# Column sums of head and layer norms in float32r from split sources, the split a stage ahead

## The chip, the cores and the metric

The kernel runs on one core of a Trainium2 chip. The metric is the device time of one execution in microseconds. Five engines work beside each other, each through its own instructions in a fixed order: TensorE (PE, matrix products), VectorE (DVE), ScalarE (ACT), GpSimd (POOL) and SyncE (SP, which issues transfers). Semaphores join them.

## The reference, cut to what matters

One step of a decoder layer, for 512 prompt tokens and 8 samples (520 columns), in float32. The norms that the change touches are these:

```
qa = rms_norm(qa.reshape(bsz, t, A_HEADS, 2, A_HD), lw['a_qnorm_g'])      # 4 heads x 2 x 64
ka = rms_norm(ka.reshape(bsz, t, A_HEADS, 2, A_HD), lw['a_knorm_g'])
o = diff_attention(...)                                                   # 4 heads, values of 128
o = rms_norm(o, lw['a_subln_g']) * (1.0 - lam_init)
yc = silu(layer_norm(conv_c, lw['c_ln_g'], lw['c_ln_b'])) @ lw['w_c_out'] # 256 channels
dvn = layer_norm(dv, lw['d_ln_g'], lw['d_ln_b'])                          # 256 channels
q = rms_norm((h2 @ lw['w_xq'])..., lw['x_qnorm_g'])                       # cross attention, 4 heads of 128
mk = rms_norm((mem_n @ w_xk)..., x_knorm_g)                               # 4 heads, 256 memory rows
```

Around them stand the products with w_in, w_o, w_up and w_down, the attention over the prompt, a paged attention of the samples over 2048 past tokens, two convolutions and a gated branch.

## The kernel before

Channels lie on the 128 partitions and tokens along the free axis, so a norm sums over partitions. That is a product on TensorE: `colsum` multiplies a matrix of ones (`ones`, or `blk` with two blocks of 64) in float32 with the squares, for two halves of 260 columns, and every partition gets the sum. `rsqrt` (L249 to L255) makes the reciprocal deviation of it with four ACT and two DVE instructions.

The large products are float32r in three passes: each weight tile is split in a high part (`wh`, a cast on ACT, L179) and a low part (`wl`, a subtraction on DVE, L180), each activation likewise by `hilo` (L143 and L144). A tile of 128 output channels is 48 products of 260 columns (L219, into one of only two PSUM tiles `g`). The weights' tiles come as one stream, and the work on the results is written as generators: each `yield` ends a stage, and `advance` moves all that are under way by one stage behind every tile of the stream. So the order on each engine is set when the program is made: a tile's 48 products, then the small products of the stages that are due, then the next tile.

For a head norm, stage one empties the `g` tile with a multiplication (L433, `zmul`) and squares on ACT (L438, `square`), and stage two sums (L242), makes `rsqrt`, scales (L444) and splits q or k for the attention. `values` (L646 to L656) does the same for the attention's output with 256 columns (sum at L653), `post_mk` for the memory's keys (sum at L1081). `branch_c` and `branch_d` are layer norms: `center` (L785, L787) subtracts the mean from two tiles and squares, a yield, then the variance. `decode` mixes in the paged products: at L500 four products of 32 columns of weights each for one page, one for each head, and L549 for the values. L702 writes a head's queries for it (`qz`). L1196 does the same for the samples in cross attention, from `xz`.

Of the kernel before, what the change touches and what calls it, by code (L numbers as in the profile page):

```python
# [17 lines left out]
P = 128  # L18
D = 1024
NT = 520          # tokens: 512 of the prompt, then 8 samples  # L20
NP = 512
NS = 8
H2 = 260          # half of the tokens, one PSUM bank each
# [14 lines left out]
TB = 10  # L38
SLOPES = [2.0 ** (-2.0 * (i + 1)) for i in range(4)]

# order of the column tiles of w_in in the stream (tile = 128 columns)
ZQ, ZK, ZV, ZBX, ZBB, ZBC, ZCA, ZCG, ZDU, ZDV, ZG = 0, 4, 8, 12, 14, 16, 18, 20, 22, 24, 26

# columns of the packed per-partition vectors
# [10 lines left out]
# columns of the packed constants  # L55
# [40 lines left out]
def layer(ctx: ExitStack, tc: tile.TileContext, I: dict, O: dict):  # L96
# [12 lines left out]
    # ---------------------------------------------------------------- helpers  # L109
# [31 lines left out]
    def hilo(src, hi, lo):  # L141
        """hi + lo = src exactly; hi is rounded to what one pass of the tensor engine carries."""
        S.copy(hi, src)  # L143
        V.tensor_tensor(out=lo, in0=src, in1=f(hi), op=ALU.subtract)  # L144
# [20 lines left out]
    def weights(name, i):  # L165
        """the split column tile i of a matrix; the next one of the stream is begun first."""
        while len(ahead) < LA and order:
            ahead.append((order[-1], split_weights(*order.pop())))
        (n, j), w = ahead.pop(0)
        assert (n, j) == (name, i), (n, j, name, i)  # L170
        return w
# [11 lines left out]
    def first_weights():  # L183
        """the first tile of the stream, in parts that come between those of x"""
        j = order.pop()
        src = I[j[0]][j[1]].rearrange("p (k c) -> p k c", k=KT)
        w = wp.tile([P, KT, P], F32, tag="w", name="w", bufs=WB[0])
        wh = wp.tile([P, KT, P], F32R, tag="wh", name="wh", bufs=WB[1])
        wl = wp.tile([P, KT, P], F32R, tag="wl", name="wl", bufs=WB[2])
        ahead.append((j, (wh, wl)))  # L190
        n = KT // PARTS
        parts = [slice(i * n, i * n + n) for i in range(PARTS)]
        for sl in parts:
            SP.dma_start(out=w[:, sl], in_=src[:, sl])
            yield
        for sl in parts:
            tc.keep_in_program_order(S.copy(wh[:, sl], w[:, sl]))
            free.add(V.tensor_tensor(out=wl[:, sl], in0=w[:, sl], in1=f(wh)[:, sl], op=ALU.subtract).ins.name)
            yield
# [3 lines left out]
    def pin():  # L203
        """what VectorE has been given since the last sums were taken up stays behind that."""
        traced = nc.cur_bb.bb.instructions
        if evac[0] is not None:
            for i in traced[evac[1]:]:
                if i.engine == evac[0].engine and i.name not in free and i is not evac[0]:
                    tc.add_manual_dep(i, evac[0].name, mybir.DependencyInfo(
                        mybir.DependencyClass.NoSync, mybir.DependencyReason.DATA), reason="pin")  # L210
        evac[1] = len(traced)
# [3 lines left out]
    def mm3(outs, wh, wl, xh, xl, first, last):  # L215
        """outs: [(psum region, moving slice)], adds w^T x in three passes."""
        for n, (w, x) in enumerate(((wh, xh), (wh, xl), (wl, xh))):
            for o, sl in outs:
                m = PE.matmul(o, lhsT=w, rhs=x[sl], start=first and n == 0, stop=last and n == 2)  # L219
        return m  # L220
# [7 lines left out]
    def gemm(ps, W, xs, first=True, last=True, k0=0, apart=False):  # L228
        """both halves of the tokens; apart: one after the other"""
# [6 lines left out]
    def colsum(mat, srcs):  # L236
        """mat^T (sum of srcs over partitions) in float32: two halves with their columns."""
        out = []
        for sl in (slice(0, H2), slice(H2, NT)):
            ps = mtile()  # L240
            for i, s in enumerate(srcs):
                PE.matmul(ps[:, 0:H2], lhsT=mat, rhs=s[:, sl], start=i == 0, stop=i == len(srcs) - 1)  # L242
            out.append((ps[:, 0:H2], sl))
        return out

    def rsqrt(src, n, v, y, a):
        """v = (src / n + EPS) ** -0.5, with one Newton step: v (3 - x v^2) / 2."""
# [19 lines left out]
    def rstd(mat, srcs, n, y, v=None):  # L267
        """the reciprocal deviations from column sums; y is scratch."""
        v, a = v if v is not None else T(), T()
        rsqrt(colsum(mat, srcs), n, v, y, a[:, 0:NT])  # L270
        return v

    # ---------------------------------------------------------------- constants
# [15 lines left out]
    ident, ones, blk = cv("ident"), cv("ones"), cv("blk")  # L289

    # ---------------------------------------------------------------- x: split, norm
# [5 lines left out]
    for i in range(WARM):          # the array's clock rises while the first loads come in  # L297
# [45 lines left out]
    def parameters():  # L343
        """the little columns made from the parameters"""
# [20 lines left out]
    # ---------------------------------------------------------------- the stream of products  # L365
    pending, flows, fresh = [], [], [False]

    def behind():
        """keeps a product that waits for others out of the way of the column tiles before it."""
        return tc.issue_after(PE_last[0].ins)  # L370

    def onward(ps):
        """a stage of each, behind the newest column tile; returns those that go on"""
# [3 lines left out]
    def advance():  # L377
        """the newest sums are taken up, then what is left of the older ones goes a stage on."""
# [10 lines left out]
    def go():  # L389
        """a stage of everything"""  # L390
# [6 lines left out]
    def flush():  # L397
        """everything that is left"""
# [3 lines left out]
    def take(post):  # L402
        """what follows on a tile's sums is begun behind the next tile."""
# [5 lines left out]
    def run(name, i, src, post, steps=0, k0=0, W=None, apart=False):  # L409
        """one column tile"""  # L410
# [7 lines left out]
    def pair(names, src, posts):  # L418
        """the first two column tiles, together while the rows of src come in"""
# [16 lines left out]
    def square(z):  # L436
        sq = T()
        S.activation(sq, z, AF.Square)  # L438
        return sq

    def headnorm(z, sq, mat, n, g):
        """z * g * rsqrt(mean over the rows of mat's blocks)"""
        y = rstd(mat, [sq], n, sq)
# [15 lines left out]
    # ---------------------------------------------------------------- paged decode attention  # L459
    last = []  # L460

    def fetch(dst, src, i):
        """dst = the page that entry i of the page table names."""
# [9 lines left out]
    def decode():  # L473
# [33 lines left out]
        # the new token's own score  # L507
# [76 lines left out]
    # ---------------------------------------------------------------- attention over the prompt  # L584
    def scores(h, qts):
        """the scores of 128 queries each; the two halves of a head in banks of their own"""
# [14 lines left out]
    def difference(h, qt, ps):  # L601
        """of the two softmaxes"""
# [20 lines left out]
    def turned(h, qt, d):  # L623
        """the keys of one tile of queries on the partitions"""
# [13 lines left out]
    def values(h, pr, dh, dl):  # L638
        """times v, and the norm of the head"""
# [10 lines left out]
        S.activation(sq[:, 0:256], ps[:, 0:256], AF.Square)  # L650
        yield
        ps = mtile()
        PE.matmul(ps[:, 0:256], lhsT=ones, rhs=sq[:, 0:256], start=True, stop=True)  # L653
# [9 lines left out]
    def attention():  # L663
        """a stage a tile: the scores of some queries, the turning of those before, their values, their norm"""
# [18 lines left out]
    def post_q(h):  # L683
        def post(ps):
# [9 lines left out]
            qn = headnorm(z, sq, blk, 64, sc[:, 0:1])  # L694
# [10 lines left out]
    def post_k(h):  # L705
        def post(ps):
# [3 lines left out]
            kn = headnorm(z, sq, blk, 64, col("gk"))  # L710
# [25 lines left out]
    # ---------------------------------------------------------------- branch B  # L736
# [43 lines left out]
    def center(ys, ps):  # L780
        """subtracts the mean over the 256 channels of two tiles; returns the squares."""
# [7 lines left out]
        return sq  # L789

    # ---------------------------------------------------------------- branch C
# [51 lines left out]
    # ---------------------------------------------------------------- branch D  # L843
    def sigmoid(y, x, scale=1.0):
        """between exponentials, whose table is called back"""
# [22 lines left out]
    def branch_d():  # L868
        sq = center(dv, colsum(ones, dv))
        yield  # L870
        r = rstd(ones, sq, 256, sq[0])
# [65 lines left out]
    def branch_c():  # L937
        convstep(31)
        lnexp()
        sq = center(yc, colsum(ones, yc))  # L940
        yield
        r = rstd(ones, sq, 256, sq[0])
# [13 lines left out]
    # ---------------------------------------------------------------- gates and merge  # L956
# [85 lines left out]
    # ---------------------------------------------------------------- memory K/V of the prompt  # L1042
# [31 lines left out]
    def post_mk(h):  # L1074
        def post(ps):
            t, sq = T(), T()
            V.tensor_tensor(out=t[:, 0:256], in0=ps[:, 0, 0:256], in1=Rm, op=ALU.mult)
            S.activation(sq[:, 0:256], t[:, 0:256], AF.Square)
            yield
            ps = mtile()  # L1080
            PE.matmul(ps[:, 0:256], lhsT=ones, rhs=sq[:, 0:256], start=True, stop=True)  # L1081
# [21 lines left out]
    def memvalues(q):  # L1103
        """a quarter of the products for the values of all heads, the tokens on the partitions"""
# [25 lines left out]
    # ---------------------------------------------------------------- w_o, first residual  # L1130
    def residual(c, ps, base, acc, g):
        """x = base + ps; its split times the gain g; its squares into acc."""
# [30 lines left out]
    # ---------------------------------------------------------------- cross attention  # L1163
# [6 lines left out]
    def post_xq(h):  # L1170
        def post(ps):
# [14 lines left out]
            qn = headnorm(z, sq, ones, 128, sc[:, 2:3])  # L1186
# [24 lines left out]
    def samples():  # L1211
        """the samples against their memories"""
# [36 lines left out]
    def cross(h):  # L1249
        """the prompt against its memory"""  # L1250
# [67 lines left out]
    # ---------------------------------------------------------------- FFN  # L1318
# [56 lines left out]
def pack(inp):  # L1375
    g = {k: np.asarray(v) for k, v in inp.items()}

    def tiles(w, ct, kt):
        """[kt*128, ct*128] -> [ct, 128 rows, kt*128]"""
# [87 lines left out]
```

## Time and profile before

| | us |
|---|---|
| three runs | 1077.41, 1075.08, 1074.6 |
| median | 1075.08 |
| span of the profiled execution | 1072.4 |
| TensorE busy in it | 1062.6 |
| VectorE busy | 594.8 |
| ScalarE busy | 457.7 |

The span runs from the first to the last instruction of the profiled execution, whose time with what lies around it is not listed apart. Busy times are sums over the engine's instructions, so an engine can be busy for a small share of the span and still be late in one stage. The granted clock of TensorE was 0.999 over the span.

### The profile page before, as it was taken

What the parts mean: (1) busy time and instruction counts of PE and PEld (TensorE: products, weight loads), DVE (VectorE), ACT (ScalarE), POOL (GpSimd) and SP (SyncE); (2) the same over time, 40 slices, a digit from 0 to 9 for tenths busy, and PEclk for the clock granted to TensorE, in tenths of its full rate; (3) what the DMA queues carried; (4) which work ended last, traced back from release to release, by engine and by line L of the source; (5) the groups of instructions that cost most, each with busy time, mean ns of one, the idle gap of its engine ahead of it and who ended that gap; (6) DMA issues with size and microseconds to landing.
All of it is one profiled execution on the core that took longest, in us unless ns stands there. A gap on an engine that the chain in (4) does not pass through costs nothing.

```text
span 1072.4 us, 21375 instructions
## 1 busy us (share of the span) xinstructions
PE 1062.6 (99%) x8434; PEld 962.0 (90%) x8434; DVE 594.8 (55%) x1022; ACT 457.7 (43%) x761; POOL 4.4 (0%) x11
## 2 busy tenths in 40 slices
PE   8999999999999999999999999999999999999998
PEld 7967777878988888888999986999999999999998
DVE  6764665775646665534677678754224424445443
ACT  7754565863412225312555586553223213312320
POOL 0000000000000000000010000000000000000000
PEclk9999999999999999999999999999999999999999
DMA  8667777756567777766432556122232232222231
GB/s 280 239 193 215 218 209 221 237 172 181 178 206 237 236 218 235 218 206 216 148 132 86 202 188 239 41 99 91 87 99 90 90 99 86 93 99 82 96 110 50
DMA packets 73861, 172.06 MB, mean 160 GB/s; under 512 B 9633, under 2 KB 12450, under 8 KB 73634
## 3 DMA queue, kind: packets, MB, share of 16 engines
q1 hardware_dynamic: 73442, 169.65, 50.1%
q8 instruction: 66, 1.08, 0.4%
q0 software_dynamic: 320, 1.07, 0.3%
q14 instruction: 33, 0.27, 0.1%
HBM read 165.07 MB, written 5.61 MB: 159 GB/s over the span
## 4 chain that ended last, share of the span: by engine, by line
PE 96%; ACT 1%; DVE 1%; DMA 0%; SPq 0%; issue 0%; DVEq 0%
PE g L219 80%; PE d L500 4%; PE d L549 3%; PE m L242 2%; PE m L597 1%; PE m L219 1%; PE g L1115 1%; PE m L646 1%; PE m L632 0%; PE m L653 0%; DMA hl<-in_xT 0%; PE m L1261 0%; PE d L1196 0%; ACT t L1266 0%; PE m L730 0%; PE m L534 0%
## 5 line engine op out<-in xcount | busy, mean ns | idle before, releaser
L219 PE MATMUL g<-hl,wh 128*128 128x260 f32 x4332 | 709.2, 285 | 1.2 <-ACT hl L324 0.6
L219 PEld LDWEIGHTS g<-hl,wh 128*128 128x128 f32 x4332 | 595.5, 188 | 51.6 <-issue 18.6
L219 PE MATMUL g<-hl,wl 128*128 128x260 f32 x2166 | 437.0, 283 | 0.0
L219 PEld LDWEIGHTS g<-hl,wl 128*128 128x128 f32 x2166 | 334.1, 188 | 1.9 <-issue 1.7
L179 ACT CAST wh<-w 128x1024 fp32r<-128x1024 f32 x154 | 161.4, 1048 | 395.4 <-PE g L219 309.0
L180 DVE TENSOR_TENSOR wl<-w,wh 128x1024 fp32r<-128x1024 f32 x154 | 188.1, 1222 | 160.9 <-ACT wh L179 151.8
L433 DVE TENSOR_TENSOR t<-g,R 128x520 f32<-128x520 f32 x48 | 33.4, 696 | 76.3 <-PE g L219 76.2
L219 PE MATMUL g<-hb,wh 128*128 128x260 f32 (+1 forms) x436 | 71.1, 282 | 0.0
L219 PEld LDWEIGHTS g<-hb,wh 128*128 128x128 f32 x436 | 60.8, 188 | 0.1
L219 PE MATMUL g<-hb,wl 128*128 128x260 f32 (+1 forms) x218 | 46.6, 283 | 0.0
L500 PE MATMUL d<-pg,qz 128*32 128x512 f32 x256 | 44.9, 604 | 0.4 <-DVE qz L702 0.4
L143 ACT CAST hl<-t 128x520 fp32r<-128x520 f32 (+2 forms) x42 | 24.4, 581 | 43.2 <-DVE t L1331 27.5
L827 DVE SCALAR_TENSOR_TENSOR hl<-uc,cols,hl 128x512 f32<-128x512 f32 x60 | 41.4, 745 | 0.0
L1345 DVE TENSOR_TENSOR hb<-g,hb 128x520 f32<-128x520 f32 x16 | 11.2, 700 | 49.4 <-PE g L219 49.4
L144 DVE TENSOR_TENSOR hl<-t,hl 128x520 fp32r<-128x520 f32 (+2 forms) x42 | 27.0, 644 | 15.8 <-ACT hl L143 15.5
L219 PEld LDWEIGHTS g<-hb,wl 128*128 128x128 f32 x218 | 34.6, 188 | 0.0
L549 PE MATMUL d<-pg,Dt 128*32 128x512 f32 x256 | 33.9, 604 | 0.0
L249 ACT ACTIVATE t<-m,little 128x260 f32<-128x260 f32 (+1 forms) x42 | 19.1, 474 | 26.1 <-PE m L242 13.2
L965 ACT ACTIVATE t<-t 128x520 f32<-128x520 f32 x24 | 15.2, 635 | 27.1 <-DVE t L433 27.0
L254 DVE TENSOR_TENSOR t<-t 128x520 f32<-128x520 f32 (+1 forms) x27 | 15.5, 576 | 19.5 <-ACT t L253 19.1
L1331 DVE TENSOR_TENSOR t<-t 128x520 f32<-128x520 f32 x32 | 22.2, 694 | 0.0
L608 DVE CUSTOM_DVE_ANT_0 t<-m,bias 128x128 f32<-128x128 f32 (+3 forms) x32 | 14.6, 486 | 12.3 <-PE m L597 12.3
(271 smaller groups left out, 818.3 us busy)
## 6 DMA issues: line engine op xcount, KB each, us to landing
pg<-in_kc SPq DMA_DIRECT2D x128, 256.0 KB, 3.4
pg<-in_vc SPq DMA_DIRECT2D x128, 256.0 KB, 3.0
w<-in_win SPq DMA_DIRECT2D x56, 512.0 KB, 4.5
w<-in_wup SPq DMA_DIRECT2D x32, 512.0 KB, 3.3
w<-in_wdn SPq DMA_DIRECT2D x32, 512.0 KB, 3.3
w<-in_wo SPq DMA_DIRECT2D x8, 512.0 KB, 3.3
hl<-in_cmk SPq DMA_DIRECT2D x16, 256.0 KB, 5.2
hl<-in_cmv SPq DMA_DIRECT2D x16, 256.0 KB, 5.5
```

The lines of the kernel that those rows point to most:

```text
L143: S.copy(hi, src)
L144: V.tensor_tensor(out=lo, in0=src, in1=f(hi), op=ALU.subtract)
L179: S.copy(wh, w)
L180: free.add(V.tensor_tensor(out=wl, in0=w, in1=f(wh), op=ALU.subtract).ins.name)
L219: m = PE.matmul(o, lhsT=w, rhs=x[sl], start=first and n == 0, stop=last and n == 2)
L242: PE.matmul(ps[:, 0:H2], lhsT=mat, rhs=s[:, sl], start=i == 0, stop=i == len(srcs) - 1)
L249: S.activation(v[:, sl], i, AF.Identity, scale=-1.0 / n, bias=NEPS)
L433: V.tensor_tensor(out=two(t), in0=gv(ps), in1=two(Rt), op=ALU.mult)
L500: PE.matmul(ps[32 * h:32 * h + 32, :], lhsT=qz[:, s * 128 + 32 * h:s * 128 + 32 * h + 32], rhs=kp[:, :, h * P:h * P + P], start=s == 0, st ...
L549: PE.matmul(ps[32 * i:32 * i + 32, :], lhsT=Dt[:, n % 16, :], rhs=vp[:, i, :], start=n % 16 == 0, stop=n % 16 == 15)
L827: V.scalar_tensor_tensor(out=y[:, 0:NP], in0=u[:, k:k + NP], scalar=cw[:, k:k + 1], in1=y[:, 0:NP], op0=ALU.mult, op1=ALU.add)
L1331: V.tensor_tensor(out=r, in0=r, in1=r, op=ALU.mult)
```

## The change

Sources of the sums are split in a high and a low float32r tile (`split`), and the sum adds two float32r products (`splitsum`, `squaresum`) with float32r copies of the two matrices. The split is written before the yield, so that it belongs to the stage ahead of the sum. In `branch_c` and `branch_d` the two tiles are split too, and a yield stands between that and the mean, so that a layer norm takes one stage more. The ring of scratch tiles grows from 10 to 15, and the scratch that is reserved for GpSimd's transfers becomes smaller. The sums of the first norm, of the norms behind w_o and before w_up, of the memory's rows and of the samples stay in float32.

```
-TB = 10
+TB = 15
...
+    def split(t, n=NT):
+
+        hi, lo = T(F32R), T(F32R)
+        hilo(t[:, 0:n], hi[:, 0:n], lo[:, 0:n])
+        return hi, lo
+
+    def splitsum(mat, parts):
+
+        out = []
+        for sl in (slice(0, H2), slice(H2, NT)):
+            ps = mtile()
+            for i, s in enumerate(parts):
+                PE.matmul(ps[:, 0:H2], lhsT=mat, rhs=s[:, sl], start=i == 0, stop=i == len(parts) - 1)
+            out.append((ps[:, 0:H2], sl))
+        return out
+
+    def squaresum(parts):
+
+        ps = mtile()
+        for i, s in enumerate(parts):
+            PE.matmul(ps[:, 0:256], lhsT=onesr, rhs=s[:, 0:256], start=i == 0, stop=i == 1)
+        return ps
...
-        rsqrt(colsum(mat, srcs), n, v, y, a[:, 0:NT])
+        rsqrt((colsum if mat is ones else splitsum)(mat, srcs), n, v, y, a[:, 0:NT])
...
+    onesr = cst.tile([P, P], F32R, name="onesr")
+    blkr = cst.tile([P, P], F32R, name="blkr")
...
+        V.tensor_copy(onesr, ones)
+        V.tensor_copy(blkr, blk)
...
         S.activation(sq, z, AF.Square)
-        return sq
+        return (sq, *split(sq))
...
-        y = rstd(mat, [sq], n, sq)
+        y = rstd(mat, sq[1:], n, sq[0])
...
         S.activation(sq[:, 0:256], ps[:, 0:256], AF.Square)
-        yield
-        ps = mtile()
-        PE.matmul(ps[:, 0:256], lhsT=ones, rhs=sq[:, 0:256], start=True, stop=True)
+        parts = split(sq, 256)
+        yield
+        ps = squaresum(parts)
...
-            qn = headnorm(z, sq, blk, 64, sc[:, 0:1])
+            qn = headnorm(z, sq, blkr, 64, sc[:, 0:1])
...
-        return sq
+        return sq, [p for s in sq for p in split(s)]
...
     def branch_d():
-        sq = center(dv, colsum(ones, dv))
-        yield
-        r = rstd(ones, sq, 256, sq[0])
+        parts = [p for t in dv for p in split(t)]
+        yield
+        sq, parts = center(dv, splitsum(onesr, parts))
+        yield
+        r = rstd(onesr, parts, 256, sq[0])
...
-    nc = _bacc.Bacc("TRN2", target_bir_lowering=False, num_devices=1)
+    nc = _bacc.Bacc("TRN2", target_bir_lowering=False, num_devices=1, dynamic_dma_scratch_size=2048)
```

`branch_c` changes as `branch_d` does, `post_mk` as `values`, k and the q of cross attention as q. Lines of the changed kernel are some 22 to 31 higher: the evacuation L433 is L460 there, L444 is L471, the sums are L258 and L266.

On VectorE, among the head norms near 45 us, the multiplication that empties the tile of head 0's k (`g_548`) stood here. `wl` is a weight's low part, `hl` the low part of a normed q, `qnew` and `qz` the samples' queries:

```order
L180 TENSOR_TENSOR wl_694<-w_691,wh_693 128x1024
L254 TENSOR_TENSOR t_608<-t_608,t_607 128x520
L255 SCALAR_TENSOR_TENSOR t_607<-t_608,t_503 128x520
L444 SCALAR_TENSOR_TENSOR t_397<-t_397,sc_197,t_607 128x520
L433 TENSOR_TENSOR t_745<-g_548,R_214 128x520
```

With the change the same tile is called `g_566` and the same multiplication is L460:

```order
L144 TENSOR_TENSOR t_626<-t_623,t_625 128x520
L144 TENSOR_TENSOR hl_510<-t_327,hl_509 128x512
L180 TENSOR_TENSOR wl_720<-w_717,wh_719 128x1024
L277 TENSOR_TENSOR t_630<-t_630,t_629 128x520
L278 SCALAR_TENSOR_TENSOR t_629<-t_630,t_517 128x520
L471 SCALAR_TENSOR_TENSOR t_399<-t_399,sc_199,t_629 128x520
L180 TENSOR_TENSOR wl_806<-w_803,wh_805 128x1024
L144 TENSOR_TENSOR hl_646<-t_399,hl_645 128x512
L725 COPY qnew_215<-t_399 128x8
L729 COPY qz_210<-t_399 64x8 x2
L460 TENSOR_TENSOR t_771<-g_566,R_216 128x520
```

The next weight's split, the split of head 1's q and its copies now stand ahead of the emptying of the tile, and `t_626`, the low half of the squares of head 3, ahead of all of it.

On ScalarE in branch D, near 215 us, the value of a head is copied and squared (L649, L650), then the two tiles of the branch are squared (L787):

```order
L649 COPY t_3523<-m_3516 128x256
L650 ACTIVATE t_3524<-m_3516 128x256
L787 ACTIVATE t_3543<-hl_2342 128x520
L787 ACTIVATE t_3547<-hl_2607 128x520
L179 CAST wh_3697<-w_3695 128x1024
L249 ACTIVATE t_3608<-m_3606,little_79 128x256
```

With the change, `hl_2402` and `hl_2668` are the two tiles of the branch, and the copy and the square are L676 and L677:

```order
L676 COPY t_3605<-m_3598 128x256
L677 ACTIVATE t_3606<-m_3598 128x256
L179 CAST wh_3632<-w_3630 128x1024
L143 CAST t_3609<-t_3606 128x256
L179 CAST wh_3783<-w_3781 128x1024
L143 CAST hl_3236<-t_3435 128x256
L143 CAST t_3621<-hl_2402 128x520
L661 CAST dh_3613<-m_3702 128x4x128
L143 CAST t_3625<-hl_2668 128x520
L272 ACTIVATE t_3689<-m_3686,little_79 128x256
```

A weight cast now stands between the square and the cast of its high part, and the casts of the branch's tiles behind another one; their squares come a stage later. TensorE had there, behind a tile's 48 products, one page product, the value's sum, four transposes, the sums of the branch and three page products:

```order
L500 MATMUL d<-pg,qz 32x512
L653 MATMUL m<-t,cc 128x256
L632 MATMUL m<-cc,t 128x128 x4
L242 MATMUL m<-t,cc 128x260 x4
L500 MATMUL d<-pg,qz 32x512 x3
```

With the change:

```order
L527 MATMUL d<-pg,qz 32x512 x4
L266 MATMUL m<-t,onesr 128x256
L659 MATMUL m<-cc,t 128x128 x4
L266 MATMUL m<-t,onesr 128x256
L258 MATMUL m<-t,onesr 128x260 x8
```

The four page products now stand together, and the sums at L258 are the means, where the variances stood.

In cross attention, near 634 us, TensorE had the eight sample products of head 1 in a row, between products of values (L1115) and of attention (L1261):

```order
L1115 MATMUL g<-wh,hb 128x512 x2
L1196 MATMUL d<-hl,xz 32x256 x8
L1261 MATMUL m<-hb,hl 128x256 x2
L1279 MATMUL m<-cc,t 128x128 x4
```

With the change they are L1227, and the transposes L1310:

```order
L1227 MATMUL d<-hl,xz 32x256 x2
L1310 MATMUL m<-cc,t 128x128
L1227 MATMUL d<-hl,xz 32x256
L1310 MATMUL m<-cc,t 128x128
L1227 MATMUL d<-hl,xz 32x256 x5
```

They now come as two, one and five with transposes between. Head 2's come as five, one, one and one in the same way.

## Rows read from the trace of the kernel before

**Rows 1.** The page: busy time of each engine; the last chain by engine.

```profile
PE 1062.6 (99%) x8434; PEld 962.0 (90%) x8434; DVE 594.8 (55%) x1022; ACT 457.7 (43%) x761; POOL 4.4 (0%) x11
...
PE 96%; ACT 1%; DVE 1%; DMA 0%; SPq 0%; issue 0%; DVEq 0%
```

**Rows 2.** Waits of TensorE by line and releaser: us in total, times, longest.

```profile
PE m L1279 <- DVE t L1270: 0.9, 1, 0.9
```

**Rows 3.** Windows: busy us of each engine, granted clock, share of transfers, GB/s.

```profile
40.00:60.00 20.00, 19.61 (x146) 16.36 (x145) 17.74 (x36) 17.00 (x29) 0.00 (x0) 1.00 0.41 138
200.00:220.00 20.00, 20.00 (x143) 17.16 (x141) 15.37 (x33) 18.97 (x38) 0.00 (x0) 1.00 0.60 204
400.00:420.00 20.00, 20.00 (x159) 17.22 (x152) 15.11 (x23) 8.98 (x11) 0.00 (x0) 1.00 0.75 229
640.00:660.00 20.00, 18.12 (x132) 13.67 (x134) 17.66 (x39) 15.74 (x37) 0.00 (x0) 1.00 0.85 310
```

**Rows 4.** The last chain, 30 to 62 us: start, us, what.

```profile
33.73 5.74 PE g L219 x48
...
46.97 0.88 PE m L242 x4
...
54.47 0.99 PE d L500 x6
...
55.85 2.76 PE d L500 x18
```

**Rows 5.** Records of the float32 sums by line: ns shortest, median and longest.

```profile
L242 PE MATMUL m<-t,cc x64: 380/382/487, 32.7 to 640.5; 128*128 128x260 f32 x64
...
L242 PE MATMUL m<-hl,cc x20: 380/382/487, 19.8 to 417.6; 128*128 128x260 f32 x20
...
L653 PE MATMUL m<-t,cc x16: 377/379/483, 99.9 to 236.8; 128*128 128x256 f32 x16
...
L1081 PE MATMUL m<-t,cc x8: 378/379/454, 605.0 to 659.1; 128*128 128x256 f32 x8
```

**Rows 6.** Casts and subtractions of splits that are there before, by form.

```profile
L143 ACT CAST hl<-t x42: 388/623/632, 40.5 to 1008.4; 128x520 fp32r<-128x520 f32 x22, 128x512 fp32r<-128x512 f32 x12, 128x256 fp32r<-128x256 f32 x8
...
L144 DVE TENSOR_TENSOR hl<-t,hl x42: 417/696/703, 41.2 to 1009.0; 128x520 fp32r<-128x520 f32 x22, 128x512 fp32r<-128x512 f32 x12, 128x256 fp32r<-128x256 f32 x8
```

**Rows 7.** Timeline of VectorE, 30 to 52 us: start, us, what.

```profile
46.62 0.69 DVE L433 TENSOR_TENSOR t<-g,R 128x520 f32<-128x520 f32 x1
```

**Rows 8.** The last chain, 195 to 240 us.

```profile
210.07 0.88 PE m L242 x4
...
212.02 0.99 PE m L242 x4
...
215.76 0.98 PE d L500 x2
...
219.55 0.99 PE d L500 x6
220.54 5.94 PE g L219 x48
226.48 1.35 PE m L646 x12
...
237.20 1.02 PE m L891 x16
238.22 0.99 PE d L500 x8
```

**Rows 9.** Timeline of all engines, 214.9 to 217.3 us.

```profile
215.19 0.39 ACT L650 ACTIVATE t<-m 128x256 f32<-128x256 f32 x1
...
216.66 0.70 PE L653 MATMUL m<-t,cc 128*128 128x256 f32 x2
```

**Rows 10.** The last chain, 590 to 715 us.

```profile
624.33 1.00 PE d L1196 x16
```

**Rows 11.** A window at the start, columns as in rows 3.

```profile
0.00:3.00 3.00, 1.48 (x2) 0.84 (x3) 0.58 (x3) 1.28 (x1) 1.29 (x6) 1.00 0.22 38
```

More of the change, by code (lines that the diff above doesn't have):

```diff
@@ L709, in post @@
             yield
-            kn = headnorm(z, sq, blk, 64, col("gk"))
+            kn = headnorm(z, sq, blkr, 64, col("gk"))
             SP.dma_start(out=O["kT"][h], in_=kn)
@@ L939, in branch_c @@
         lnexp()
-        sq = center(yc, colsum(ones, yc))
+        parts = [p for t in yc for p in split(t)]
         yield
-        r = rstd(ones, sq, 256, sq[0])
+        sq, parts = center(yc, splitsum(onesr, parts))
+        yield
+        r = rstd(onesr, parts, 256, sq[0])
         for c in range(2):
@@ L1078, in post @@
             S.activation(sq[:, 0:256], t[:, 0:256], AF.Square)
+            parts = split(sq, 256)
             yield
-            ps = mtile()
-            PE.matmul(ps[:, 0:256], lhsT=ones, rhs=sq[:, 0:256], start=True, stop=True)
+            ps = squaresum(parts)
             v, a = T(), T()
@@ L1185, in post @@
             yield
-            qn = headnorm(z, sq, ones, 128, sc[:, 2:3])
+            qn = headnorm(z, sq, onesr, 128, sc[:, 2:3])
             for r in range(2):
```

## The prediction

> **What bounds the kernel now.** The head of the profile comes first: TensorE is busy 1062.6 of 1072.4 us, VectorE for 55% and ScalarE for 43%, and the chain that ended last is 96% TensorE [rows 1]. The list of TensorE's waits says the same from the other side: behind the first microseconds its longest is 0.9 us, in cross attention [rows 2]. So a microsecond less on TensorE is a microsecond off the end, as long as VectorE and ScalarE deliver in time. The windows say where that is in doubt: these engines are at 17.7 and 17.0 of 20 us at the head norms, ScalarE is at 19.0 around branch D, and VectorE at 17.7 again in cross attention [rows 3]. The time before is the median 1075.08; the profiled span of 1072.4 lies 2.7 below it, and I add my sum to the median as it is.
>
> **What it removes: 10.3 us of TensorE.** The chain shows a head norm's sums (q3's, at 46.97) as four float32 records in 0.88 us, 0.22 each; 48 float32r products of the same 260 columns take 5.74, 0.12 each [rows 4]. Each float32 sum is two records; split, it is two float32r products, so each pair of records of 260 columns becomes 0.24 instead of 0.44. The records are counted by line [rows 5]: 64 of head norms and variances at L242, 16 of the 20 with hl (the means of C and D; four belong to the first norm and stay), 16 at L653 and 8 at L1081. That is 80 x 0.10 = 8.0, and 24 records of 256 columns at 0.215 to 0.12, another 2.3.
>
> **What it adds: 32 casts and 32 subtractions.** 20 are of 520 columns, 12 of 256. Rows of just these forms stand in the trace: the cast 0.39 to 0.63 us, the subtraction 0.42 to 0.70 [rows 6]. So ScalarE gets some 20 x 0.63 + 12 x 0.40 = 17 us and VectorE 20 x 0.70 + 12 x 0.42 = 19 us more, beside TensorE's 1062. Where the tile products cover them they are free; I laid the rows of the three engines end to end in the new order, stage by stage, with the durations of the trace. The two copies of constants and the larger ring (the pairs need their slots back only after sums that are long done) cost nothing in this; the smaller scratch for GpSimd's transfers neither, as four loads use it long ahead. Bounds for these: 0 to 1 us.
>
> **26 to 62 us, head norms: +1.6.** VectorE empties k0's tile from 46.62 to 47.31 [rows 7], and the next product, k1's, which needs that bank, starts at 46.97 + 0.88 = 47.85, behind q3's sums [rows 4]: 0.5 us of slack. In the new order there stand ahead of it, besides, a weight split (1.22), two subtractions (0.69 each) and the copies of head 1 (0.5), less what starts earlier: some 3.0, so it ends at about 50.3. TensorE arrives at 46.97 - 3 x 0.40 + 0.48 + 0.4 (two short waits for q3's evacuation and a low half) = 46.65 and waits 3.7. The product starts at 50.4 instead of 47.85 (+2.55), k0's sums give back 0.40, and the page products took 4.14 in before, from 54.47 to 58.61 with 0.39 of waiting for head 3 between their two pieces [rows 4]; three steps of 0.92 to 0.99 are 2.97 if head 3 comes in time. By the rows it comes 0.5 us behind the first three, which leaves some 3.6: +1.6 in all. If all of this wait were hidden it would be -2.0; if the page products wait as before, +2.2.
>
> **62 to 195 us: -2.2.** Three k heads at 0.40 and five value norms at 0.19. No row of TensorE's waits lies here and the tile products cover the casts; bound above: if all of VectorE's 3.6 us of subtractions (three at 0.62 start to start, five at 0.34) came onto the path, +1.4.
>
> **Branch D, 195 to 240 us: +1.35.** Here the cover is thin. TensorE comes to the second value's sum at 216.66 [rows 9]. From this go 0.88 + 0.99 (the means, now a stage later), 0.97 (page products near 197 that are no longer cut in two) and 0.19 (the first value's sum) [rows 8]: 213.6. ScalarE squares that value up to 215.58 [rows 9]; this comes 0.8 earlier, but a weight cast (1.04) and the new cast (0.41) follow before the sum: 216.1, a wait of 2.5. The low half stands behind a weight split: 0.7 more. The means need the split of both dv, which stand behind one more weight cast and two others: 220.2, a wait of 2.7. From there: means 0.96, tile product 5.94, values 1.35, variance 0.96, pages 0.99, product 5.94, sum 0.24, then 0.98, 1.02 and 0.99 [rows 8], which is 239.55 where before had 239.21 and had also done the first run of L891, 1.02 [rows 8]. So 5.9 of waits against 1.6 + 0.6 of sums and 1.9 of something else: four page products of one step run together in 0.99, but 1 + 3 of them in 0.98 + 0.99 [rows 8], and the new order cuts this two times less. Bounds: no wait, -4.1; every chain a fifth longer, +3.5.
>
> **Branch C, 400 to 435 us: -1.6.** 16 records at 0.10; VectorE and ScalarE have 4.9 and 11.0 us free of 20 there [rows 3].
>
> **Cross attention, 600 to 690 us: +1.3.** Sums -2.4 (four heads, four mk). Laying the rows gives seven waits of 0.1 to 0.5 us, 2.0 together: for low halves, for the copies into xz and for the scores' normalised rows, all on VectorE. And the new order cuts the sample products: eight in a row take 1.00 [rows 10], in two rounds of four; heads 1 and 2 now have them as 2, 1, 5 and 5, 1, 1, 1, with transposes between, so three and five rounds at 0.45 to 0.5: +2.1, of which I let 0.4 fill the waits. Bounds: -2.4 and +4.5.
>
> Sum: 1.6 - 2.2 + 1.35 - 1.6 + 1.3 = +0.45, so **1075.5 us**.
>
> **Rivals.** (a) *The waits don't come, the removed work shows.* Speaks for it: that TensorE's waits are under 1 us behind the start [rows 2], with the other engines as full as they are. With half of my waits (5.8 of 11.6) gone it is 1069.7, with all 1063.9. Speaks against: 0.5 us of slack at 46.62 is a row, and 3 us go before it.
>
> (b) *VectorE becomes the bound of the busy stages.* The place is 62 to 195 and 605 to 660: if each new subtraction there delays the next evacuation, 3.6 and 4.4 us come onto the path instead of 0 and 2.0: +6.0, 1081.5. It decides from the point at which VectorE has under 0.6 us free per 5.75-us tile. Speaks for it: 17.66 of 20 us [rows 3]. Against: a tile of 62 to 195 us brings one pair at most, 0.6 of 5.75 us, and even at branch D VectorE has 4.6 of 20 us free [rows 3].
>
> (c) *TensorE's clock falls in the new waits.* [...]
>
> (d) *float32r sums are not cheaper.* Then 10.3 comes back: 1085.8. Against it stand 48 products of the same columns in 5.74 [rows 4].
>
> **How the numbers follow.** Forecast 0.40, with its own range of 1072 to 1079.5; (a) 0.29; (b) 0.19; (c) 0.10; (d) 0.02. A measurement of this kernel tells 0.3%, 3.2 us, from nothing. Faster is (a) and a little of the forecast's lower edge, 0.31; the same is most of the forecast and of (a)'s and (b)'s weak forms, 0.39; slower 0.30. The range takes the half of (a) and goes through (b) into (c): 1067 to 1083.
>
> **What would show it.** Right, if the profile after has: sums at 0.12 per record; a wait of 3 to 4 us of TensorE near 47 to 50 us for the evacuation of k0; waits of 2 to 3 us each for the cast of a value's squares near 214 and for a low half near 218 to 220; no wait from 62 to 190 and at branch C; sample products (L1196, L1227 after the change) in pieces of 0.5 us. Wrong, if the waits near 47 or near 215 are below 1 us (then rival a), if TensorE waits for VectorE in most tiles from 62 to 195 (b), if the granted clock of a window is below 1.00 (c), or if the new sums take 0.2 per record (d).

## The result, and the profile after

The changed kernel takes 1083.3 us (1081.92 to 1085.46, four runs) where the kernel before takes 1075.24: ratio 1.0072, interval 1.0055 to 1.0089. It is slower, by 8 us. The forecast was 1075.5 within 1067 to 1083, so the time stands 0.3 above the top of the range, less than its own runs differ, and the likeliest case was not the one that came. The profiled execution of the changed kernel spans 1081.2 us, 8.8 more than that of before.

The page of the changed kernel, busy times and the last chain:

```profile
PE 1060.0 (98%) x8434; PEld 961.1 (89%) x8434; DVE 611.0 (57%) x1056; ACT 474.9 (44%) x793; POOL 4.4 (0%) x11
...
PE 89%; DVE 4%; ACT 4%; DMA 2%; SPq 1%; issue 1%; DVEq 0%
```

ScalarE has 17.2 us more work and VectorE 16.2, as forecast (17 and 19). TensorE has only 2.6 less where 10.3 of sums were taken out (what fills the rest comes below), and the last chain, 96% TensorE in before [rows 1], now runs through other engines for a tenth. The list of TensorE's waits, where before had nothing above 0.9 behind its start [rows 2]:

```profile
PE g L219 <- DVE t L460: 5.1, 3, 3.9
PE m L1310 <- DVE t L1301: 2.3, 1, 2.3
PE m L266 <- DVE t L683: 2.0, 1, 2.0
...
PE m L258 <- DVE t L144: 1.4, 1, 1.4
PE m L266 <- DVE s L1257: 1.4, 1, 1.4
PE m L266 <- DVE t L144: 0.7, 1, 0.7
PE m L266 <- DVE dl L662: 0.7, 1, 0.7
```

The windows of the changed kernel around the three places of these waits (columns as in [rows 3], the granted clock behind POOL):

```profile
46.00:50.00 4.00, 0.85 (x8) 0.64 (x6) 3.90 (x9) 3.64 (x6) 0.00 (x0) 1.00 0.35 129
50.00:54.00 4.00, 3.30 (x16) 3.33 (x17) 3.68 (x9) 3.32 (x7) 0.00 (x0) 0.57 0.36 127
...
216.00:220.00 4.00, 1.30 (x10) 0.70 (x6) 3.63 (x7) 4.00 (x9) 0.00 (x0) 1.00 0.80 255
220.00:224.00 4.00, 2.60 (x10) 2.18 (x11) 4.00 (x7) 2.85 (x7) 0.00 (x0) 0.61 0.87 259
224.00:228.00 4.00, 4.00 (x22) 4.00 (x21) 3.29 (x10) 2.63 (x5) 0.00 (x0) 0.53 0.39 146
...
660.00:664.00 4.00, 1.14 (x10) 0.75 (x9) 3.70 (x10) 3.36 (x12) 0.00 (x0) 1.00 0.77 314
664.00:668.00 4.00, 2.65 (x14) 1.73 (x18) 3.89 (x7) 3.42 (x7) 0.00 (x0) 0.58 0.37 131
668.00:672.00 4.00, 4.00 (x14) 1.42 (x7) 3.90 (x7) 1.94 (x5) 0.00 (x0) 0.57 0.52 179
```

TensorE idles for most of the first window of each place (3.2, 2.7 and 2.9 of 4 us), at a clock still granted in full (1.00), and in the windows behind that the clock is 0.53 to 0.61. In windows of 1 us it is 0.50 from 51 to 53, from 221 to 227 and from 665 to 671 us. Before had 1.00 in every window of 4 us up to 1068 us.

Where the time goes shows when the same product is compared in both traces, at points with the same work behind them. Its start, in us, from the timelines of TensorE (the fifth point is the first product of the values, L1115 before and L1146 after, the others are tile products):

| product | before | after | difference | step | forecast |
|---|---|---|---|---|---|
| behind the first page products | 58.54 | 61.12 | +2.6 | +2.6 | +1.6 |
| behind branch D | 253.03 | 258.88 | +5.9 | +3.3 | -0.85 |
| behind branch C | 431.85 | 436.19 | +4.3 | -1.5 | -1.6 |
| before cross attention | 598.17 | 602.38 | +4.2 | -0.1 | 0 |
| in its first part | 631.31 | 633.93 | +2.6 | -1.6 | |
| behind it | 684.83 | 694.36 | +9.5 | +6.9 | together +1.3 |
| span | 1072.4 | 1081.2 | +8.8 | -0.7 | 0 |

The head norms in the chain of the changed kernel, 25 to 70 us (start, us, what):

```profile
49.86 0.71 DVE t L460
...
50.70 7.29 PE g L219 x48
58.00 0.48 PE m L258 x4
58.48 2.71 PE d L527 x24
```

The evacuation of k0's tile comes at 49.86 (forecast 49.6), the product behind it waited 3.86 (forecast 3.7), and four sums take 0.48 instead of 0.88 [rows 4]. But the 48 products take 7.29 instead of 5.74, with the clock at 0.57 from 50 to 54 us. At branch D, in the chain from 190 to 245 us, the same: 7.45 instead of 5.94 [rows 8], and seven records of the means, at the low clock too (0.50 from 222 to 224 us), 2.06, where eight take 1.00 a stage later, at a clock of 1.00 (232 to 234 us):

```profile
221.97 2.06 PE m L258 x7
224.03 7.45 PE g L219 x48
231.48 1.35 PE m L673 x12
232.83 1.00 PE m L258 x8
```

In cross attention (600 to 730 us) the sample products of head 1 are cut as the order said, and those of the memory's values behind the third wait are slow: ten records in 3.55 with the clock at 0.50 (667 to 671 us), sixteen in 1.88 at 1.00 (677 to 679 us). These are five products and eight, and three take 0.99 at 1.00 (at 675.51): by these times five are two rounds as eight are, an estimate.

```profile
637.79 0.56 PE d L1227 x4
...
638.60 0.55 PE d L1227 x2
...
639.41 0.98 PE d L1227 x10
...
666.51 0.77 PE m L266 x2
667.28 3.55 PE d L1264 x10
...
677.29 1.88 PE d L1264 x16
```

Behind a wait of 0.7 us two records at L266 take longer with the clock at 1.00 too (207 to 209 us): 0.48, where they take 0.24 without a wait, also at 1.00 (240 to 241 us).

```profile
207.86 0.48 PE m L266 x2
...
240.78 0.24 PE m L266 x2
```

Read from these rows, the clock costs some 1.3 us at the first place (7.29 against 5.98 in an experiment below, in which the product starts at the same time), 1.5 + 1.1 at branch D, and 1.7 + 0.3 in cross attention (3.55 against some 1.88, 0.77 against 0.48): an estimate of 5.9 of the 8.8.

### The profile page after: what moved, and what is told of

Its sections match the earlier page's. It is cut to its first block, busy times and chain, and to the rows that moved or that the text cites. A ratio compares the mean times of both kernels' runs of the same rounds, so it can differ in the third digit from the quotient of the medians.

```text
span 1081.2 us, 21427 instructions
## 1 busy us (share of the span) xinstructions
PE 1060.0 (98%) x8434; PEld 961.1 (89%) x8434; DVE 611.0 (57%) x1056; ACT 474.9 (44%) x793; POOL 4.4 (0%) x11
## 3 DMA queue, kind: packets, MB, share of 16 engines
q1 hardware_dynamic: 73442, 169.65, 49.6%
## 4 chain that ended last, share of the span: by engine, by line
PE 89%; DVE 4%; ACT 4%; DMA 2%; SPq 1%; issue 1%; DVEq 0%
PE g L219 75%; PE d L576 3%; PE d L527 3%; PE m L219 1%; DMA w<-in_win 1%; PE g L1146 1%; DVE wl L180 1%; PE m L624 1%; PE m L258 1%; ACT wh L179 1%; PE d L1227 1%; PE d L1264 1%; PE m L673 1%; PE m L1292 1%; DMA hl<-in_xT 0%
## 5 line engine op out<-in xcount | busy, mean ns | idle before, releaser
L460 DVE TENSOR_TENSOR t<-g,R 128x520 f32<-128x520 f32 x48 | 33.4, 695 | 75.2 <-PE g L219 75.2
L143 ACT CAST hl<-t 128x520 fp32r<-128x520 f32 (+2 forms) x42 | 24.4, 582 | 46.8 <-DVE t L1362 27.6
L527 PE MATMUL d<-pg,qz 128*32 128x512 f32 x256 | 41.6, 603 | 0.0
L144 DVE TENSOR_TENSOR hl<-t,hl 128x520 fp32r<-128x520 f32 (+2 forms) x42 | 26.9, 643 | 15.3 <-ACT hl L143 15.0
L640 ACT ACTIVATE t<-t,s 128x128 f32<-128x128 f32 (+3 forms) x32 | 17.7, 554 | 4.7 <-DVE s L638 4.5
```

The source lines that it names most:

```text
L460: V.tensor_tensor(out=two(t), in0=gv(ps), in1=two(Rt), op=ALU.mult)
L527: PE.matmul(ps[32 * h:32 * h + 32, :], lhsT=qz[:, s * 128 + 32 * h:s * 128 + 32 * h + 32], rhs=kp[:, :, h * P:h * P + P], start=s == 0, st ...
L640: S.activation(pj[j][:, 0:n], pj[j][:, 0:n], AF.Exp, bias=st[:, 2 + j:3 + j], accum_out=st[:, 4 + j:5 + j])
```

## The experiments

The theories: **A**, each long wait of TensorE lets its clock fall, and this is most of the loss; **B**, the clock matters little, and the work added to VectorE and ScalarE is paid everywhere. The kernel before was timed beside each group: 1076.34, 1075.76 and 1076.66 us.

**One place undone at a time.** First the q heads:

```
-            sq = square(z)                            # post_q
+            sq = square(z, False)
-            qn = headnorm(z, sq, blkr, 64, sc[:, 0:1])
+            qn = headnorm(z, sq, blk, 64, sc[:, 0:1])
```

> The changed kernel with the four q heads' sums back in float32 and their splits left out. [...] Theory B (the clock falls by itself or costs nothing; the added work of VectorE and ScalarE is what is paid): the clock is still 0.5 somewhere near 50 us, the time 1082 to 1083.

Measured: 1084.26 (ratio 1.0069, 1.0050 to 1.0088). This is above what either theory said: A had 1080.5, with the wait of 3.9 us near 47 us and the low clock behind it gone, B 1082 to 1083. The wait and the low clock at 50 us are gone, but nothing is won. The order of the page products differs: the tile behind the first of them starts at 55.42, with 6 of their records done where both other kernels have done 24, so most of that lead is work put off. Up to 208 us TensorE then waits 1.8 us for pages, 0.9 for a value and twice 0.5 for other results, and the lead is gone (208.03, and 208.37 in the changed kernel). At branch D it now waits once for 4.3 us, and near 294 us its clock falls (0.83 from 292 to 296 us) where that of the changed kernel did not (1.00; 60 products in 8.79 us instead of 7.27). Its windows and the wait at D:

```profile
50.00:54.00 4.00, 4.00 (x36) 4.00 (x35) 3.96 (x9) 2.67 (x6) 0.00 (x0) 1.00 0.36 131
...
220.00:224.00 4.00, 2.94 (x10) 2.14 (x10) 4.00 (x8) 2.97 (x8) 0.00 (x0) 0.50 0.82 255
```

```profile
PE m L266 <- ACT t L143: 4.3, 1, 4.3
```

So A was right on the clock at the first place and wrong on the time: other waits took the place of the one that went. How much of that is due to the other order of the page products the run does not show.

Then branch D:

```
-        parts = [p for t in dv for p in split(t)]
-        yield
-        sq, parts = center(dv, splitsum(onesr, parts))
-        yield
-        r = rstd(onesr, parts, 256, sq[0])
+        sq, _ = center(dv, colsum(ones, dv), False)
+        yield
+        r = rstd(ones, sq, 256, sq[0])
```

> The changed kernel with branch D alone as it was: float32 sums, no split, no extra stage. Theory A: no stretch at clock 0.5 near 222 us, no wait above 1 us there, and the 4.2 us that the changed kernel loses between 206 and 253 us are gone: 1079.3. Theory B: the waits go, but the clock has no part in it: some 1.4 us less, 1082.

Measured: 1081.47 (1.0048, 1.0030 to 1.0066). The clock is 1.00 from 220 to 228 us; from the tile at 207 to that at 253 us it takes 46.2, as before (46.2), where the changed kernel took 50.5: 4.3 back, as A says. The time is between the theories: it lies 5.1 us above the kernel before timed beside it, where the changed kernel lay 8.1 above its own. In the profiled execution 3.1 of the 4.3 went at another place, near 290 us, of which more below (60 products take 9.77 us there, 7.27 in the changed kernel):

```profile
220.00:224.00 4.00, 3.20 (x16) 2.08 (x15) 3.58 (x6) 3.90 (x10) 0.00 (x0) 1.00 0.74 211
...
292.00:296.00 4.00, 4.00 (x20) 4.00 (x20) 2.07 (x4) 1.05 (x1) 0.00 (x0) 0.50 0.83 206
```

Then cross attention, `square(z, False)` and `ones` in `post_xq`, the sum of `post_mk` as before:

> The changed kernel with cross attention (xq and mk) back in float32. Theory A: the waits of 2.3, 0.6 and 1.4 us near 660 us and the 6.8 us at clock 0.5 behind them are gone, the eight sample products stand together again; the 5.3 us lost between 600 and 680 us go: 1078.0. Theory B: 1081 or more.

Measured: 1078.45 (1.0021, 1.0011 to 1.0030), 4.9 below the changed kernel, as A says. From the tile at 598 to that at 685 it takes 86.6 (before 86.7, changed 92.0), and the clock stays at 1.00 from 660 to 672 us:

```profile
664.00:668.00 4.00, 3.12 (x21) 1.20 (x21) 3.92 (x6) 3.94 (x9) 0.00 (x0) 1.00 0.45 145
```

**The waits filled with idle products.**

```
+        if (name, i) == ("win", ZK + 1):
+            spare = dtile()
+            with behind():
+                for _ in range(14):
+                    PE.matmul(spare, lhsT=onesr, rhs=src[0][0][:, 0:512], start=True, stop=True)
         gemm(ps, W, src, k0=k0, apart=apart)
...
+    def idlework(ps, n, src):
+        for _ in range(n):
+            PE.matmul(ps[:, 0:256], lhsT=onesr, rhs=src[:, 0:256], start=True, stop=True)
```

> The changed kernel with idle products of TensorE (their results are overwritten) in its three long waits: 14 of 512 columns near 47 us, 26 of 256 near 214 to 220 us, 28 of 256 near 660 us. Nothing else is changed, except that page products near them fall into other places. Theory A: the granted clock stays at 1.00 there, and the tile behind the first wait takes 5.75 instead of 7.29 us; 7 us come back, less up to 2 where the idle products don't fit the waits: 1077, 1075.5 to 1079. Theory B: the time stays at 1083 or rises.

Measured: 1088.61 (1.0118, 1.0100 to 1.0137): by the time B was right, and as an improvement it failed. In cross attention the idle products themselves waited 2.8 us (L265, by the list for VectorE's L144), and the clock still fell (0.78 from 668 to 672 us); the page products were cut more; how the 5 us above the changed kernel divide was not worked out. At branch D the clock stayed at 1.00 from 216 to 228 us. And at the first place it is the cleanest test of A. The tile product starts at 50.78 (50.70 in the changed kernel), with TensorE busy until shortly before:

```profile
46.00:50.00 4.00, 4.00 (x22) 3.21 (x20) 3.90 (x9) 3.73 (x6) 0.00 (x0) 1.00 0.33 126
50.00:54.00 4.00, 3.34 (x28) 3.25 (x28) 3.71 (x8) 3.25 (x7) 0.00 (x0) 1.00 0.40 132
```

```profile
50.78 5.98 PE g L219 x48
```

A clock of 1.00 and 5.98 us instead of 0.57 and 7.29, with TensorE busy for all of the 4 us from 46 to 50 instead of 0.85 of them: here the low clock goes with the idling.

**Only covered places converted.** q, D and cross attention undone together, in one kernel with the value norms, in the other without:

> Only branch C, the four k heads and the eight value norms keep the new sums; q, branch D and cross attention are as in the kernel before. Theory A (the loss is the waits at the three busy places and the clock behind them): no wait above 1 us for a split, no stretch at clock 0.5 near 50, 222 and 665 us; sums 4.7 us less, four cuts of page products less and one more (-2.9), waits of 1 to 2: 1069, 1067.5 to 1071.5. Theory B (VectorE's and ScalarE's added work is paid everywhere): 1074 or more.

> As the kernel with branch C, the k heads and the values converted, but the values too are left in float32. Sums 3.2 us less than in the kernel before, one cut of page products less and one more: 1072, 1070.5 to 1073.5. Beside that other kernel it tells what the values' splits are worth between 62 and 200 us: 1.5 us of sums if their waits cost nothing (theory A), nothing or a loss if they do (theory B).

Measured: 1076.18 (1.0007, 0.9997 to 1.0018) and 1074.25 (0.9989, 0.9979 to 0.9999). The first misses A's 1069 by 7 us and is where B put it, the second misses its 1072 by 2. The one long wait of the first is again in the stage of branch D, though D itself is as before: it is the split of a value's squares,

```profile
PE m L266 <- ACT t L143: 2.4, 1, 2.4
```

and behind it the clock falls (0.50 from 220 to 224 us). From the tile at 207 to that at 253 us it takes 50.0 instead of 46.2. Without the values' splits that stage takes 46.8. So in these two kernels a value's split in that stage costs more than eight value sums save.

**The splits left out.**

```
-        sq = T()
+        sq = T(F32R)
         S.activation(sq, z, AF.Square)
-        return (sq, *split(sq))
+        return T(), sq
```

> The squares are rounded to float32r as ScalarE writes them, and the sums take this one product: the low half of each square is left out, and with it every added cast and subtraction; the means of C and D stay in float32 in their old stage. Theory A: no wait of TensorE above 1.5 us behind the start, clock 1.00 at all three places; sums -10.3 + 1.6 for the means - 5.2 for the second product, page products cut about one time more: 1062, 1060 to 1065. Theory B (float32r sums, the ring or the order cost by themselves): 1070 or more.

Measured: 1071.55 (0.9961, 0.9947 to 0.9975): 4.2 us faster than before instead of the 14 that A expected. Without any added cast or subtraction TensorE still waits, 2.0 us for k0's evacuation and 2.3 us in cross attention, and its clock is at 0.64 from 50 to 54 us:

```profile
PE m L1306 <- DVE t L1297: 2.3, 1, 2.3
PE g L219 <- DVE t L460: 2.0, 1, 2.0
```

This corrects A: in the kernel before, the chains of VectorE and ScalarE end about when TensorE needs them, 0.5 us ahead at the head norms [rows 4], [rows 7] and 0.9 us late in cross attention [rows 2]. A faster sum there turns into waiting even when nothing is added for it, and the clock was lower here too: 0.64 from 50 to 54 us, 0.94 from 660 to 664 us.

**The ring and the scratch alone**, `TB = 15` and `dynamic_dma_scratch_size=2048` in the kernel before:

> The kernel before with the ring of 15 scratch tiles and the smaller scratch for GpSimd's transfers, nothing else; TensorE's order is the same. Both theories: 1075.5, within 1.5 us of the kernel before. A third, that these two cost part of the 8 us: 1078 or more.

Measured: 1075.37 (0.9998, 0.9989 to 1.0008): nothing. The run gives something else. TensorE's instructions stand in the same order as in the kernel before, and 60 products behind 16 narrow ones (L534, 32 columns) take 1.4 us longer. This kernel's chain:

```profile
284.69 3.49 PE m L534 x32
288.18 0.38 PE m L538 x2
288.56 8.64 PE g L219 x60
```

The kernel before there:

```profile
284.56 3.49 PE m L534 x32
288.05 0.22 PE m L538 x2
288.27 7.27 PE g L219 x60
```

Its clock is 0.57 from 288 to 292 us, that of before 1.00. And it is 0.57 once more in cross attention, from 660 to 664 us, where before again had 1.00 and waits of 0.9, 0.6 and 0.4 us stand in its list; TensorE is busy for 3.59 of these 4 us, 3.53 in before:

```profile
660.00:664.00 4.00, 3.59 (x19) 1.10 (x18) 3.92 (x6) 3.74 (x8) 0.00 (x0) 0.57 0.43 142
```

So at both places the clock fell in the one execution (0.57) and not in the other (1.00), where TensorE's order is the same.

**Branch C alone**, the rest as before:

> The kernel before with branch C alone converted (its split, the extra stage and the two sums), and the larger ring; TensorE's order differs from the kernel before in the two places of C alone. Theory A: 16 sums of 0.44 become 32 products of 0.12, 1.6 us less, no wait at C: 1074.2 where the kernel before has 1075.7, if both have the same falls of the clock. Theory B (the added casts and subtractions are paid here too): 1075.7 or more.

Measured: 1073.61 (0.9970, 0.9960 to 0.9980), the fastest of all that compute the whole. From the tile at 414 to that at 432 us it takes 15.8 instead of 17.4: 1.6, as forecast. The rest of the 3 us between the medians is not explained by C; one fall of the clock more or less, 1.4 us near 288 us, would be of that size, which is not shown.

**The mean of D in its old stage**, `sq, parts = center(dv, colsum(ones, dv))` in the changed kernel:

> The changed kernel, but branch D takes its means in float32 in their old stage: no split of dv and no extra stage, the variance still from split squares. TensorE's order differs from the changed kernel's at D alone. Theory A: the wait for the split of dv (1.4 us) goes; the waits for the value's split squares (2.0 and 0.7) stay, and if they let the clock fall it falls for less; of the 4.2 us lost between 206 and 253 us some 2.5 come back, in all 1081. If the extra stage alone were the cause: all 4.2, 1079.

Measured: 1085.86 (1.0084, 1.0069 to 1.0100). This is 2.6 above the changed kernel, where A said 1081 and the extra stage as the cause 1079. From the tile at 207 to that at 253 us it takes 50.4, as with the extra stage (50.5). TensorE now waits 0.5 and 0.7 us for the value's squares (2.0 and 0.7 in the changed kernel) and 1.0 and 0.4 for the variance's, and the clock falls (0.50 from 224 to 228 us; five records of the variance take 1.45 there). The tile product behind them:

```profile
226.87 7.58 PE g L219 x48
```

So the loss in this stage needs neither the extra stage nor the split of dv. With branch D undone the value's split had the same waits of 0.5 and 0.7 and the clock stayed (1.00 from 216 to 228 us), so here the low clock comes with the split of the variance's squares.

## Why the prediction was right and wrong

**The removed work** was right: 0.48 for four sums, 0.24 for two of 256 columns, 0.96 for eight. It shows in full at branch C (-1.5 of -1.6), the one place with slack on both other engines [rows 3], and in the first part of cross attention (-1.6, which is the sums of three heads at 0.40 and of two mk at 0.19).

**26 to 62 us** was right in its mechanism and in the size of the wait (3.86 for 3.7). The page products cost less than thought (2.71 for 3.6); the tile product started 0.3 later and takes 5.98 behind a wait where 5.74 was laid; and the clock cost 1.3: +2.6 for +1.6.

**62 to 253 us** was wrong: +3.3 for -2.2 + 1.35. Of the 4.1 between, 2.6 are the clock at branch D. The waits there came where they were put, but 1.8 shorter in all (2.0 for the split square, 0.7 for its low half, 1.4 for the means; forecast 2.5, 0.7, 2.7). The list of waits puts the first down to VectorE's L683, which writes nothing that the sum reads; the cast of the square's high half on ScalarE ended at 218.35, with it:

```profile
217.94 0.41 ACT L143 CAST t<-t 128x256 fp32r<-128x256 f32 x1
```

In the stretch up to 208 us that was costed at no wait TensorE idled some 1.6 more, among it 0.8 for an evacuation near 178 us and 0.7 for a value near 208. That leaves 1.7, of which some 1 is the slower start behind four of the waits (an estimate, at the 0.24 that the records at L266 and the tile product at 5.98 take longer). The forecast of branch D did not agree with itself either: 5.9 of waits less 1.6, 0.6 and 1.9 is +1.8, where its other sum gave +1.35.

**Cross attention** was wrong: +5.3 for +1.3. The cut sample products cost 2.7 (0.56 + 0.55 + 0.98, then 0.98 and three of 0.55, against 1.00 each) for 2.1: 2, 1 and 5 take four rounds, not the three that were counted. The waits grew by 2.1 over those of before (as forecast, 2.0, but most of it in one place of 4.3 behind 660 us, not in seven small ones), and the clock cost 2.0. Some 0.9 has no row.

**The step that failed** is rival (c): the clock stood beside the forecast at a chance of 0.10 and was no term of the sum, because no row of before showed a wait of 4 us or its price. It came at all three places, with 1.3 to 2.6 us each and 5.9 together by the estimate above; its sign, a window below 1.00, came too (0.53 to 0.61). The top of the range, 1083, goes into (c), and no row of before shows the price that this takes; the runs showed 1.3, 2.6 and 2.0 us in its place. Forecast plus the clock is 1081.4; the other 2 us are the waits of 62 to 208 us, the sample products and the slower starts, less the shorter waits at branch D and the page products. The waits were in the forecast itself, and the runs show what came with the first of them: 0.57 behind the wait of 3.9 us, 1.00 where the wait was filled. Rivals (a), (b) and (d) did not come: the waits are there, TensorE doesn't wait in most tiles from 62 to 195 us, and the sums are cheap.

A silent assumption failed too, as the kernel without low halves shows: that what TensorE saves ahead of a busy stage is kept unless the added work delays it. At the head norms and in cross attention the saving became waiting even with nothing added.

## What to carry to other kernels

Taking work from the engine that bounds the whole pays in full only in stages where the others have slack: here branch C alone, with 5 and 11 us free of 20, gave its 1.6 us, while the conversion of everything lost 8. When a forecast contains new waits of TensorE of a few us, add the price of its clock to each of them at once, from a row at the low clock where there is one (here 1.3 to 2.6 us each), rather than keep it as an unlikely rival. And when a scheduler decides the order, count what it cuts apart: products of 32 columns of weights that took 1.00 us as eight in a row took 0.56, 0.55 and 0.98 here as two, one and five.

## What the runs showed of the hardware

The clock also fell where TensorE didn't idle: behind 3.49 us of products of 32 columns each, in a window where it is busy all the time, the next 4 us were granted 0.57 in one execution and 1.00 in another with the same order. The low clock shows there in the profiled executions of six experiments (lowest window of 4 us between 284 and 296 us: 0.83 with q undone and with cross attention undone, 0.50 with branch D undone, 0.63 without the splits, 0.57 with the ring and the scratch alone, 0.58 with branch C alone), not in those of the kernel before, the changed one and the one with branch C, the k heads and the values (1.00); no edit touched that place. In the pair above it cost 1.4 us. Over the runs of the kernel before, time and mean granted clock go together: 1073.9 to 1074.9 us at 0.999, 1076.5 to 1077.6 at 0.996 and 0.997. So falls of the clock fit the spread of 3 us between runs of one kernel; which places fall in which run was not traced.
